# A decoder layer on one core: first three products side by side, squares summed on VectorE alone, first norm's chain with high priority

## The chip, the cores and the metric

The kernel runs on 1 core of a Trainium2 chip. The metric is device time in microseconds (us) of one execution. The engines are TensorE (PE; PEld is its weight load), VectorE (DVE), ScalarE (ACT), GpSimd (POOL) and SyncE (SP), whose queue issues the DMAs.

## The reference

One decoder layer, batch 1, 512 tokens, width 1024, all in float32:

```python
h = rms_norm(x, norm1_g[i])
proj = h @ w_in[i]
u_s5 = proj[..., :IN_S5_END]
q = proj[..., IN_S5_END:IN_Q_END]
...
z_rw = proj[..., IN_V_END:IN_RW_END]
gate_logits = proj[..., IN_RW_END:]
y_a = s5_mixer(u_s5, ...)
y_b = diff_attention(q, k, v, ...)
y_c, v_first = rwkv7_mixer(z_rw, ...)
...
merged = jnp.sum(gates * branch_out, axis=2)
x = x + (merged @ w_out[i]).astype(x.dtype)
h2 = rms_norm(x, norm2_g[i])
gu = h2 @ w_ffn_in[i]
x = x + ((jax.nn.silu(gu[..., :D_FF]) * gu[..., D_FF:]) @ w_ffn_out[i]).astype(x.dtype)
```

with `rms_norm(x, g) = x * rsqrt(mean(x*x) + eps) * g`, the mean taken over the 1024 channels of a token.

## The kernel before

Activations lie transposed, channels on the 128 partitions and the 512 tokens along the row, so x is eight tiles of 128x512. Each float32 operand is split into a high part of type float32r and the rest: `act_hi`, `act_lo` for the activations, `wh`, `wl` for a weight block of 128x512 (four k tiles of a product with 128 output columns). A product over eight k tiles is then 24 matmuls of 128x512 into one PSUM bank: hi by `wh`, lo by `wh`, hi by `wl` (lines 1296 to 1298).

The norm's scale per token isn't in `act_hi`: only the gain is multiplied in (line 252). The products start on the unscaled x, and whoever takes a product from its bank multiplies it by `R1`, the reciprocal root spread over 128 partitions: lines 330 (RWKV inputs) and 1592 (a gate). The products of the low-rank inputs, "b" and "a", are copied out of their banks first (line 329, ACT), so that their banks come free without `R1`. The two dense banks are `bank_83` and `bank_84`, so a third product waits until one of the first two has been taken.

`R1` comes from this chain: eight squares of x on ACT (line 1506); their sum in two halves, three additions on POOL and three on DVE (line 1511), and one that joins them (line 1520); eight small matmuls with a column of ones (line 1524); the reciprocal root in small DVE steps (lines 231 to 242); a copy that spreads it (line 1526); four transposes on PE (line 1529); a copy out of PSUM on ACT (line 1572).

A weight block is loaded into one of three raw tiles `wr` (SP queue, line 1224), rounded to `wh` by ACT (line 1225), and subtracted to `wl` by DVE (line 1226); only then may its raw tile be loaded again. `load4` (lines 1242 to 1254) does so for the narrow "a" weights, whose 32 columns stand four times, the third copy being the rest; that product is `narrow`, 16 matmuls on lines 1262 and 1263.

The order of the program's steps is the text `ORDER`: L is the two low-rank products, R00 the first RWKV input (the k input of pair 0), G1 a gate, R01 and R02 the next RWKV inputs, P and T an RWKV pair's preparation and its 64x64 blocks, S, H and U the S5 mixer's steps. The code issues instructions in that order, and a scheduler then orders each engine's queue once, at build time, by its own estimate of when operands are ready; on the chip every engine runs its queue in that fixed order. The tiles `x`, the squares, and S5's working tiles all come from one list of slots (`ar_6`, `ar_12` to `ar_14` among them).

Of the kernel before, what the change touches and what calls it, by code (L numbers as in the profile page):

```python
# [23 lines left out]
P = 128  # L24
T = 512
DM = 1024
DFF = 2816
KD = DM // P
# [6 lines left out]
NSPLIT = (6, 3, 2, 3)  # L35
ORDER = ("L R00 G1 R01 R02 P0 T0 I0 R10 R12 S R11 U0 P1 R20 R22 R21 T1 H0 G1 J0 U1 I1 J1 C0 P2 T2 F0 U3 U2 Q0 C1 G3 Q1 G2 H1 I2 Q2 R31 "
         "F1 R32 R30 P3 T3 J2 G1 I3 J3 C3 G1 Q3 X0 K0 A0 G2 Y0 C2 Y1 Y2 Y3 F3 X1 K1 G1 A1 F2 X2 K2 O0 O2 O3 G2 A2 X3 K3 G3 O1 A3")
# [647 lines left out]
class S5:  # L685
# [6 lines left out]
    NJ, NK, L = 16, 64, 8  # L692
# [509 lines left out]
KB = 4  # L1202


class Dense:
# [49 lines left out]

    def narrow(self, wx, nk, hi, lo, take):

        E, nc = self.E, self.E.nc
        bank = E.dense_bank()
        for k in range(nk):  # L1260
            w = wx[k // KB][:, k % KB].rearrange("p g n -> p (g n)")
            nc.tensor.matmul(bank, w, hi(k), start=k == 0, stop=False)
            nc.tensor.matmul(bank, w, lo(k), start=False, stop=k == nk - 1)
        take(bank)
        E.free(bank)

# [268 lines left out]
def trunk_kernel(ctx: ExitStack, tc: tile.TileContext, A, outT):  # L1535
# [13 lines left out]
    nc.scalar.copy(E.small("warm", [P, 1], bufs=1), E.ones)  # L1549
    norm = Rms(E, (nc.gpsimd, nc.vector))  # L1550
    with E.scope("s"):
        xs, wb = [], dense.blocks(A["w_b"], KD, P)
        for k in range(KD):
            x = E.slot("x")
            nc.sync.dma_start(x, xT[k * P:(k + 1) * P])
            E.split(x, h_hi(k), h_lo(k), E.pc("n1", k))
            xs.append(x)
            if k in (0, 2):
                dense.ahead(A["w_b"], KD, P, k // 2)
        w_a = dense.load4(A["w_a"], KD)  # L1560
        for i in range(2):
            dense.ahead(A["w_in"][4], KD, P, i)
        for k in range(KD):
            norm.add(xs[k])
# [4 lines left out]
    with E.scope("s"):  # L1569
        E.r1 = E.mpool.tile([P, 4], F32, name="r1")  # L1570
        E.R1 = E.mpool.tile([P, T], F32, name="R1")
        nc.scalar.copy(E.R1, norm(E.r1))
        E.r1sq = E.mpool.tile([P, 4], F32, name="r1sq")
        nc.vector.tensor_tensor(E.r1sq, E.r1, E.r1, ALU.mult)
# [52 lines left out]
    def lora():  # L1627
        proj(A["w_b"], lambda ps: rw.take(ps, "b"))
        dense.narrow(w_a, KD, h_hi, h_lo, lambda ps: rw.take(ps, "a"))

# [192 lines left out]
```

## Time and profile before

| what | value |
|---|---|
| median of 3 runs | 1011.51 us (1007.04 to 1014.56) |
| the profiled execution's own time | 1011.71 us |
| its span in the trace | 1009.9 us |
| PE busy | 968.3 us, 96% of the span |
| DVE busy | 753.6 us, 75% |
| ACT busy | 473.2 us, 47% |
| POOL busy | 143.8 us, 14% |

The span runs from the program's first instruction on the core to its last. PE's share is made up of matmuls that follow each other and whose ends are modelled, so 96% says that PE was seldom without work, not that it ran at its peak. A matmul's cost is best read as the distance from its start to the next one's start.

### The profile page before, as it was taken

To read this page: it belongs to the slowest core of one execution; us is meant where nothing else is said; L and a number is where in the kernel's file an instruction comes from. 1 tells how busy PE (TensorE), PEld (TensorE's weight loads), DVE (VectorE), ACT (ScalarE), POOL (GpSimd) and SP (SyncE) were. 2 spreads that over 40 slices of the span, in tenths; PEclk is the share of its full clock that TensorE was granted. 3 is DMA by queue.
4 is the path that set the end of the run, shared out by engine and by line. 5 is a ranking of instruction groups with operands and counts; after the bars stand their busy time and mean duration, and the time that the engine had idled before them with its cause. 6 is when DMAs were issued, how large, how long until landed. Compare 5 with 4: busy or idle time off the path is not lost. (4 is left out here: it accounts for less than half of the span.)

```text
span 1009.9 us, 17897 instructions
## 1 busy us (share of the span) xinstructions
PE 968.3 (96%) x6416; PEld 825.5 (82%) x6416; DVE 753.6 (75%) x1941; ACT 473.2 (47%) x978; POOL 143.8 (14%) x176
## 2 busy tenths in 40 slices
PE   6989999989999999999999899989999999999998
PEld 5767777767779787878886788889999999988886
DVE  7999666889996789977866555779989998843232
ACT  6634324424333566545455224556666666632220
POOL 3022020531420010000000332012211211000000
PEclk9999799999999999999999999989999999999999
DMA  7324252221333234252458864466667676344441
GB/s 242 116 75 112 66 121 75 74 55 53 101 106 75 79 95 126 84 157 74 152 166 282 241 206 151 143 153 159 152 160 183 143 153 169 73 149 122 136 131 37
DMA packets 105593, 129.95 MB, mean 129 GB/s; under 512 B 45376, under 2 KB 47296, under 8 KB 105504
## 3 DMA queue, kind: packets, MB, share of 16 engines
q1 hardware_dynamic: 99168, 117.28, 38.6%
q0 software_dynamic: 6336, 11.54, 7.4%
q8 instruction: 50, 0.82, 0.3%
q14 instruction: 39, 0.32, 0.1%
HBM read 109.90 MB, written 18.88 MB: 128 GB/s over the span
## 5 line engine op out<-in xcount | busy, mean ns | idle before, releaser
L1225 ACT CAST wh<-wr 128x512 fp32r<-128x512 f32 x198 | 120.3, 611 | 210.6 <-PE bank L1297 169.1
L1226 DVE TENSOR_TENSOR wl<-wr,wh 128x512 fp32r<-128x512 f32 x198 | 135.9, 689 | 81.1 <-ACT wh L1225 80.4
L1296 PE MATMUL bank<-act_hi,wh 128*128 128x512 f32 x360 | 149.3, 415 | 8.0 <-ACT wh L1225 5.9
L1297 PE MATMUL bank<-act_lo,wh 128*128 128x512 f32 x360 | 148.4, 412 | 2.0 <-DVE act_lo L253 2.0
L1298 PE MATMUL bank<-act_hi,wl 128*128 128x512 f32 x360 | 148.8, 413 | 0.0
L1385 PE MATMUL bank<-act_hi,wh 128*128 128x256 f32 x352 | 99.7, 283 | 3.4 <-ACT wh L249 3.4
L1385 PE MATMUL bank<-act_hi,wl 128*128 128x256 f32 x352 | 99.4, 283 | 0.2
L1385 PE MATMUL bank<-act_lo,wh 128*128 128x256 f32 x352 | 99.0, 282 | 0.0
L1385 PE MATMUL bank<-sp_t,wh 128*128 128x256 f32 x528 | 96.5, 283 | 0.0
L1296 PEld LDWEIGHTS bank<-act_hi,wh 128*128 128x128 f32 x360 | 69.6, 193 | 22.1 <-ACT wh L1225 5.9
L1297 PEld LDWEIGHTS bank<-act_lo,wh 128*128 128x128 f32 x360 | 69.4, 193 | 16.4 <-DVE act_lo L253 3.4
L1385 PEld LDWEIGHTS bank<-sp_t,wh 128*128 128x128 f32 x528 | 82.1, 191 | 0.0
L1298 PEld LDWEIGHTS bank<-act_hi,wl 128*128 128x128 f32 x360 | 69.4, 193 | 14.2 <-issue 0.6
L1385 PE MATMUL bank<-sp_t,wl 128*128 128x256 f32 x264 | 74.7, 283 | 0.0
L1385 PEld LDWEIGHTS bank<-act_hi,wh 128*128 128x128 f32 x352 | 67.7, 192 | 3.9 <-ACT wh L249 3.8
L1296 PE MATMUL bank<-act,wh 128*128 128x512 f32 x176 | 68.5, 389 | 0.0
L1297 PE MATMUL bank<-act,wh 128*128 128x512 f32 x176 | 68.5, 389 | 0.0
L1298 PE MATMUL bank<-act,wl 128*128 128x512 f32 x176 | 68.5, 389 | 0.0
L1385 PEld LDWEIGHTS bank<-act_hi,wl 128*128 128x128 f32 x352 | 67.4, 192 | 0.8 <-DVE wl L250 0.8
L1385 PEld LDWEIGHTS bank<-act_lo,wh 128*128 128x128 f32 x352 | 67.4, 192 | 0.0
L249 ACT CAST wh<-ar 128x512 fp32r<-128x512 f32 x79 | 48.2, 622 | 27.6 <-DMA ar<-in_w_ffn_in 13.3
L250 DVE TENSOR_TENSOR wl<-ar,wh 128x512 fp32r<-128x512 f32 x79 | 53.5, 687 | 9.1 <-ACT wh L249 7.0
(492 smaller groups left out, 2218.0 us busy)
## 6 DMA issues: line engine op xcount, KB each, us to landing
wr<-in_w_in SPq DMA_DIRECT2D x88, 256.0 KB, 3.0
ar<-in_w_ffn_in SPq DMA_DIRECT2D x46, 256.0 KB, 3.2
wr<-in_w_ffn_out SPq DMA_DIRECT2D x40, 256.0 KB, 2.7
gate<-ar SPq DMA_DIRECT2D x24, 256.0 KB, 2.5
wr<-in_w_branch SPq DMA_DIRECT2D x24, 256.0 KB, 3.3
ar<-gate SPq DMA_DIRECT2D x24, 256.0 KB, 3.4
ar<-in_w_ffn_in POOLq DMA_DIRECT2D x22, 256.0 KB, 3.9
sp_raw<-in_w_ffn_in SPq DMA_DIRECT2D x21, 256.0 KB, 3.2
```

Source lines behind the costliest of these rows:

```text
L249: nc.scalar.copy(hi, src)
L250: nc.vector.tensor_tensor(lo, src, hi.bitcast(F32), ALU.subtract)
L1225: nc.scalar.copy(wh, raw)
L1226: nc.vector.tensor_tensor(wl, raw, wh.bitcast(F32), ALU.subtract)
L1296: nc.tensor.matmul(ps, wh[:, j], hi(k), start=k == 0, stop=False)
L1297: nc.tensor.matmul(ps, wh[:, j], lo(k), start=False, stop=False)
L1298: nc.tensor.matmul(ps, wl[:, j], hi(k), start=False, stop=k == nk - 1)
L1385: nc.tensor.matmul(ps, w[x][:, c], b(y, j), start=first and j == js[0] and n == 0, stop=last and j == js[-1] and n == 2, skip_group_check= ...
```

## The change

Five edits:

- The three products of L and R00 (b, a and the k input of pair 0) run side by side in three banks: for each k tile of x there are eight matmuls, three for b, two for a, three for k. The a product takes a bank of another list, `bank_90`. Of `ORDER` only the start changes, from `L R00 G1 ...` to `L G1 ...`.
- The weights come in another order: behind the first x tile both the first b block, the a weights and the first k block; behind the fourth x tile the second b and k blocks.
- All squares are added by DVE; POOL adds none.
- The norm's chain after the sum, up to `R1`, is issued with the scheduler's highest priority.
- `narrow` goes, and `first` takes its place.

```diff
-ORDER = ("L R00 G1 R01 R02 P0 T0 I0 R10 R12 S R11 U0 P1 ...
+ORDER = ("L G1 R01 R02 P0 T0 I0 R10 R12 S R11 U0 P1 ...
...
+    def first(self, ws, wx, nk, hi, lo, takes):
+
+        nc, E = self.E.nc, self.E
+        a, b = (self.loaded.pop(repr(w)) for w in ws)
+        banks = [E.dense_bank(), E._take("ps", (P, T), True), E.dense_bank()]
         for k in range(nk):
+            q, j = k // KB, k % KB
+            first, last = k == 0, k == nk - 1
+            for bank, w in ((banks[0], a[q]), (banks[1], None), (banks[2], b[q])):
+                if w is None:
+                    x = wx[q][:, j].rearrange("p g n -> p (g n)")
+                    nc.tensor.matmul(bank, x, hi(k), start=first, stop=False)
+                    nc.tensor.matmul(bank, x, lo(k), start=False, stop=last)
+                else:
+                    nc.tensor.matmul(bank, w[0][:, j], hi(k), start=first, stop=False)
+                    nc.tensor.matmul(bank, w[0][:, j], lo(k), start=False, stop=False)
+                    nc.tensor.matmul(bank, w[1][:, j], hi(k), start=False, stop=last)
+        for bank, take in zip(banks, takes):
+            take(bank)
+            E.free(bank)
...
-    norm = Rms(E, (nc.gpsimd, nc.vector))
+    norm = Rms(E, (nc.vector,))
...
-            if k in (0, 2):
+            if k in (0, 3):
                 dense.ahead(A["w_b"], KD, P, k // 2)
-        w_a = dense.load4(A["w_a"], KD)
-        for i in range(2):
-            dense.ahead(A["w_in"][4], KD, P, i)
+                if k == 0:
+                    w_a = dense.load4(A["w_a"], KD)
+                dense.ahead(A["w_in"][4], KD, P, k // 2)
...
-        nc.scalar.copy(E.R1, norm(E.r1))
+        with tc.high_priority():
+            nc.scalar.copy(E.R1, norm(E.r1))
...
     def lora():
-        proj(A["w_b"], lambda ps: rw.take(ps, "b"))
-        dense.narrow(w_a, KD, h_hi, h_lo, lambda ps: rw.take(ps, "a"))
+
+        dense.first((A["w_b"], A["w_in"][4]), w_a, KD, h_hi, h_lo,
+                    [lambda ps: rw.take(ps, "b"), lambda ps: rw.take(ps, "a"), lambda ps: rw.take(ps, "k", 0)])
```

**PE at the start.** Before, the b product is run through and then the a product; here its end, with `wh_115` and `wl_116` the second b block and `wh_137` the first half of the a weights:

```order
L1298 MATMUL bank_83<-act_hi,wl_116 128x512
L1296 MATMUL bank_83<-act_hi,wh_115 128x512
L1297 MATMUL bank_83<-act_lo,wh_115 128x512
L1298 MATMUL bank_83<-act_hi,wl_116 128x512
L1262 MATMUL bank_84<-act_hi,wh_137 128x512
L1263 MATMUL bank_84<-act_lo,wh_137 128x512
```

Now the first rows of PE, with `wh_103` of b, `wh_110` of a and `wh_117` of k (line numbers of the changed kernel, ten or eleven higher behind `first`):

```order
L1270 MATMUL bank_83<-act_hi,wh_103 128x512
L1271 MATMUL bank_83<-act_lo,wh_103 128x512
L1272 MATMUL bank_83<-act_hi,wl_104 128x512
L1267 MATMUL bank_90<-act_hi,wh_110 128x512
L1268 MATMUL bank_90<-act_lo,wh_110 128x512
L1270 MATMUL bank_84<-act_hi,wh_117 128x512
L1271 MATMUL bank_84<-act_lo,wh_117 128x512
L1272 MATMUL bank_84<-act_hi,wl_118 128x512
```

Eight matmuls now stand on each x tile where three stood. The SP queue of the start before, where an `x8` at a row's end would be eight in a row:

```order
L1555 DMA ar_6_74<-in_xT 128x512
L1224 DMA wr_102<-in_w_b 128x512
L1555 DMA ar_6_74<-in_xT 128x512
L1555 DMA ar_12_80<-in_xT 128x512
L1224 DMA wr_114<-in_w_b 128x512
L1555 DMA ar_12_80<-in_xT 128x512 x3
L1555 DMA ar_13_81<-in_xT 128x512 x2
L1246 DMA wr_135<-in_w_a 128x256
```

The SP queue of the start now:

```order
L1565 DMA ar_6_74<-in_xT 128x512
L1224 DMA wr_102<-in_w_b 128x512
L1246 DMA wr_108<-in_w_a 128x256
L1224 DMA wr_116<-in_w_in 128x512
L1565 DMA ar_6_74<-in_xT 128x512
L1565 DMA ar_12_80<-in_xT 128x512 x2
L1224 DMA wr_102<-in_w_b 128x512
L1224 DMA wr_108<-in_w_in 128x512
L1565 DMA ar_12_80<-in_xT 128x512 x2
L1565 DMA ar_13_81<-in_xT 128x512 x2
```

The last four x tiles now stand behind two loads that use a raw tile (`wr_102`, `wr_108`) for the second time.

**DVE and ACT in the norm's chain.** DVE before, from the join of the two sums (line 1520) to the first step of the root (line 231); line 281 prepares the low-rank weights, the rest is S5's parameters:

```order
L1520 TENSOR_TENSOR ar_13_81<-ar_13_81,ar_14_82 128x512
L721 SCALAR_TENSOR_TENSOR s_r_690<-s_n_689,s_r_690 128x16
L726 TENSOR_SCALAR s_n_86_704<-s_n_689 128x16
L811 RECIPROCAL s_den_824<-s_den_824 128x16
L722 SCALAR_TENSOR_TENSOR s_r_690<-s_n_689,s_r_690 128x16
L727 TENSOR_SCALAR s_n_86_704<-s_n_86_704 128x16
L231 TENSOR_SCALAR rqx_s_178<-bank_88 128x4
L281 TENSOR_TENSOR rw_wl<-ar_1_69,rw_wl 32x1024
L233 TENSOR_SCALAR rqi_s_180<-rqx_s_178 128x4
L281 TENSOR_TENSOR rw_wl<-ar_1_69,rw_wl 32x512
```

DVE now, from the last addition (line 1521):

```order
L1521 TENSOR_TENSOR ar_13_81<-ar_13_81,ar_14_82 128x512
L281 TENSOR_TENSOR rw_wl<-ar_1_69,rw_wl 32x1024
L231 TENSOR_SCALAR rqx_s_178<-bank_88 128x4
L281 TENSOR_TENSOR rw_wl<-ar_1_69,rw_wl 32x512
L233 TENSOR_SCALAR rqi_s_180<-rqx_s_178 128x4
L1060 TENSOR_TENSOR da_pr<-da_lv 128x128
```

The long half of line 281 now stands ahead of the root's first step instead of behind it. On ACT, the rows before the copy of `R1` (line 1572) were:

```order
L1225 CAST wh_137<-wr_114 128x512
L1063 ACTIVATE da_sm<-da_sm 128x2
L1225 CAST wh_143<-wr_135 128x512
L1225 CAST wh_148<-wr_102 128x512
L1572 COPY R_172<-bank_89 128x512
```

and ahead of the same copy (line 1583) they are now:

```order
L1063 ACTIVATE da_sm<-da_sm 128x2
L329 COPY ar_7_75<-bank_90 128x512
L1225 CAST wh_117<-wr_108 128x512
L1225 CAST wh_131<-wr_116 128x512
L1225 CAST wh_136<-wr_102 128x512
L1583 COPY R_173<-bank_89 128x512
```

The copy still stands behind two weight casts whose loads are issued late, and a third cast moved behind the copy out of the a product's bank.

**PE in the second RWKV pair.** Here lines 552 and 559 are 64x64 blocks of RWKV, lines 915, 931 and 952 S5's transposes and small products. PE before:

```order
L1298 MATMUL bank_83<-act_hi,wl_140 128x512
L552 MATMUL bank_86<-ar_4_72,ar_6_74 64x64 x8
L552 MATMUL bank_86<-ar_4_72,ar_1_69 64x64 x8
L915 MATMUL bank_88<-ident,ar_14_82 128x128 x4
L931 MATMUL bank_89<-ar_14_82,s5cb_s_1788 32x128
L559 MATMUL bank_87<-ar_7_75,ar_8_76 64x32
L931 MATMUL bank_89<-ar_14_82,s5cb_s_1788 32x128 x3
L1296 MATMUL bank_84<-act_hi,wh_143 128x512
```

PE now:

```order
L1308 MATMUL bank_84<-act_hi,wl_118 128x512
L915 MATMUL bank_88<-ident,ar_13_81 128x128 x4
L915 MATMUL bank_89<-ident,ar_14_82 128x128 x4
L931 MATMUL bank_90<-ar_13_81,s5cb_s_1788 32x128 x4
L931 MATMUL bank_90<-ar_14_82,s5cb_s_1788 32x128 x4
L1306 MATMUL bank_83<-act_hi,wh_131 128x512
L1307 MATMUL bank_83<-act_lo,wh_131 128x512
L552 MATMUL bank_86<-ar_4_72,ar_6_74 64x64 x8
L552 MATMUL bank_86<-ar_4_72,ar_1_69 64x64 x8
L952 MATMUL bank_88<-ident,s_jt_874 128x128 x4
L952 MATMUL bank_89<-ident,s_jt_874 128x128 x2
```

The first of two S5 groups of lines 915 and 931, which stood far ahead of this place, has joined the second here.

## Rows read from the trace of the kernel before

**Rows 1.** The page's busy time, share of the span and instructions of each engine.

```profile
PE 968.3 (96%) x6416; PEld 825.5 (82%) x6416; DVE 753.6 (75%) x1941; ACT 473.2 (47%) x978; POOL 143.8 (14%) x176
```

**Rows 2.** Windows of 5 us: busy PE, PEld, DVE, ACT, POOL; granted clock; DMA share; GB/s.

```profile
5.00:10.00 5.00, 4.05 (x10) 2.69 (x10) 4.34 (x5) 5.00 (x10) 2.48 (x2) 1.00 1.02 355
...
40.00:45.00 5.00, 5.00 (x23) 3.99 (x22) 5.00 (x31) 1.85 (x3) 0.00 (x0) 1.00 0.22 65
```

**Rows 3.** PE in order of time: start, us, instruction, idle time before it.

```profile
5.95 0.80 PE L1296 MATMUL bank<-act_hi,wh 128*128 128x512 f32 x1 [5.95 <-ACT wh L1225]
...
9.48 0.40 PE L1298 MATMUL bank<-act_hi,wl 128*128 128x512 f32 x1
9.71 0.40 PE L1296 MATMUL bank<-act_hi,wh 128*128 128x512 f32 x1
11.40 0.50 PE L1297 MATMUL bank<-act_lo,wh 128*128 128x512 f32 x1 [1.29 <-DVE act_lo L253]
...
13.10 0.50 PE L1297 MATMUL bank<-act_lo,wh 128*128 128x512 f32 x1 [0.74 <-DVE act_lo L253]
...
20.90 0.95 PE L1524 MATMUL bank<-ones,ar 128*128 128x1 f32 x8
21.71 0.48 PE L1296 MATMUL bank<-act_hi,wh 128*128 128x512 f32 x1
...
25.99 0.40 PE L1296 MATMUL bank<-act_hi,wh 128*128 128x512 f32 x1
...
34.44 0.47 PE L1296 MATMUL bank<-act_hi,wh 128*128 128x512 f32 x1 [2.05 <-ACT ar L337]
```

**Rows 4.** ACT in order of time.

```profile
4.15 0.72 ACT L252 ACTIVATE act_hi<-ar,pcol 128x512 fp32r<-128x512 f32 x1 [1.92 <-DMA ar<-in_xT]
4.78 0.61 ACT L1506 ACTIVATE ar<-ar 128x512 f32<-128x512 f32 x1
5.29 0.60 ACT L1225 CAST wh<-wr 128x512 fp32r<-128x512 f32 x1
...
29.88 0.62 ACT L1225 CAST wh<-wr 128x512 fp32r<-128x512 f32 x1 [1.36 <-DMA wr<-in_w_in]
30.40 0.58 ACT L1572 COPY R<-bank 128x512 f32<-128x512 f32 x1
```

**Rows 5.** DVE in order of time.

```profile
8.91 1.77 DVE L1226 TENSOR_TENSOR wl<-wr,wh 128x512 fp32r<-128x512 f32 x1
...
18.94 0.69 DVE L1520 TENSOR_TENSOR ar<-ar,ar 128x512 f32<-128x512 f32 x1
...
21.88 0.16 DVE L231 TENSOR_SCALAR rqx_s<-bank 128x4 f32<-128x4 f32 x1 [1.82 <-PE bank L1524]
22.08 1.22 DVE L281 TENSOR_TENSOR rw_wl<-ar,rw_wl 32x1024 fp32r<-32x1024 f32 x1
...
27.98 0.42 DVE L1526 COPY ar<-r 128x512 f32<-128x512 f32 x1
...
33.61 0.68 DVE L1592 TENSOR_TENSOR ar<-bank,R 128x512 f32<-128x512 f32 x1
```

**Rows 6.** POOL in order of time: the second of its three additions of squares.

```profile
8.84 1.30 POOL L1511 TENSOR_TENSOR ar<-ar,ar 128x512 f32<-128x512 f32 x1 [0.40 <-ACT ar L1506]
```

**Rows 7.** Line 253 on DVE: ns min/median/max, first and last start, form.

```profile
L253 DVE SCALAR_TENSOR_TENSOR act_lo<-ar,pcol,act_hi x8: 739/744/1774, 4.9 to 14.3; 128x512 fp32r<-128x512 f32 x8
```

**Rows 8.** The eight x loads, from issue to landing.

```profile
DMA to landing us min/median/max: 2.9/4.7/5.5
```

**Rows 9.** Windows of 4 us in the second RWKV pair, columns as in rows 2.

```profile
112.00:116.00 4.00, 4.00 (x21) 2.94 (x20) 2.29 (x4) 0.58 (x1) 0.00 (x0) 0.50 0.80 194
116.00:120.00 4.00, 4.00 (x17) 3.30 (x16) 0.00 (x0) 0.66 (x2) 0.00 (x0) 0.50 0.00 0
120.00:124.00 4.00, 4.00 (x19) 2.88 (x20) 0.76 (x2) 0.83 (x2) 0.00 (x0) 0.76 0.36 81
144.00:148.00 4.00, 4.00 (x46) 3.12 (x45) 3.30 (x5) 1.18 (x2) 1.13 (x2) 1.00 0.94 185
```

More of the change, by code (lines that the diff above doesn't have):

```diff
@@ L35 @@
 NSPLIT = (6, 3, 2, 3)
-ORDER = ("L R00 G1 R01 R02 P0 T0 I0 R10 R12 S R11 U0 P1 R20 R22 R21 T1 H0 G1 J0 U1 I1 J1 C0 P2 T2 F0 U3 U2 Q0 C1 G3 Q1 G2 H1 I2 Q2 R31 "
+ORDER = ("L G1 R01 R02 P0 T0 I0 R10 R12 S R11 U0 P1 R20 R22 R21 T1 H0 G1 J0 U1 I1 J1 C0 P2 T2 F0 U3 U2 Q0 C1 G3 Q1 G2 H1 I2 Q2 R31 "
          "F1 R32 R30 P3 T3 J2 G1 I3 J3 C3 G1 Q3 X0 K0 A0 G2 Y0 C2 Y1 Y2 Y3 F3 X1 K1 G1 A1 F2 X2 K2 O0 O2 O3 G2 A2 X3 K3 G3 O1 A3")
@@ L1254, in load4 @@
         return wx
-    def narrow(self, wx, nk, hi, lo, take):
-        E, nc = self.E, self.E.nc
-        bank = E.dense_bank()
+    def first(self, ws, wx, nk, hi, lo, takes):
+        nc, E = self.E.nc, self.E
+        a, b = (self.loaded.pop(repr(w)) for w in ws)
+        banks = [E.dense_bank(), E._take("ps", (P, T), True), E.dense_bank()]
         for k in range(nk):
[L1261 to L1265, printed above, removed]
+            q, j = k // KB, k % KB
[12 more added lines that the diff above has]
+            E.free(bank)
     def tokens(self, w, nk, hi, lo, take):
@@ L1549, in trunk_kernel @@
     nc.scalar.copy(E.small("warm", [P, 1], bufs=1), E.ones)
-    norm = Rms(E, (nc.gpsimd, nc.vector))
+    norm = Rms(E, (nc.vector,))
     with E.scope("s"):
-        xs, wb = [], dense.blocks(A["w_b"], KD, P)
+        xs = []
         for k in range(KD):
```

## The prediction

> **What bounds the kernel now.** I read the page first: PE is busy for 96% of the span [rows 1], so a change can win only where PE waits or runs slowly. The change touches the first 35 us, so I went on to PE in order of time there [rows 3]. The reader is to see four losses. PE starts at 5.95 us, waiting for the first rounded weight block. From there to 9.48 us eight distances take 3.53 us, 0.44 each, where from 9.48 to 9.71 one takes 0.23: 512 columns in 0.43 us are the lower of the clock's two levels, 1.2 GHz, in 0.23 the upper, 2.4 GHz, although the granted clock of that window stands at 1.00 [rows 2]. Then come two waits for `act_lo`, 1.29 and 0.74 us. Last, at 34.44, comes a wait of 2.05 us; the trace puts it down to ACT, but PE restarts as the gate's product has been taken out of its bank, at 33.61 + 0.68 = 34.29 [rows 5]. That take needs `R1`, ready at 30.40 + 0.58 = 30.98 [rows 4], and there are 3.31 us between the two. So two things set the end of this stage: how early PE gets through b, a and k, and how early `R1` is there. Behind it VectorE is nearly full (5.00 of 5 us in a typical window, rows 2), so only a gain that both PE and VectorE get passes on.
>
> **The first products side by side.** The number of large matmuls is the same, 24 + 16 + 24 = 64. What changes is how many are ready for each x tile: eight, which take 8 x 0.233 = 1.87 us at the upper clock, where three took 0.70. ACT makes an x tile and its square in 0.63 + 0.51 = 1.14 us (the distances in rows 4), so before PE overtook it and now it can't. I rebuild the stage from these distances.
>
> ACT: the square of x0 (4.78 to 5.29) now stands behind the weight casts, so the first cast moves from 5.29 to 4.78 if its block has landed by then; PE starts between 5.95 - 0.51 = 5.44 and 5.95. I take 5.44, since the cast at 5.29 did not wait. Then three more casts and the square, 5 x 0.51 from 4.78 = 7.33, x1 at 7.96. Up to x7 there are in all 8 scalings and 10 casts and squares from 4.15: 4.15 + 8 x 0.63 + 10 x 0.51 = 14.3. `act_lo` of x7 follows 0.7 later, at 15.0.
>
> PE: 8 matmuls at the lower clock, 5.44 + 8 x 0.43 = 8.9, as x1's `act_lo` comes (7.96 + 0.7). Then 56 x 0.233 = 13.1 and the column sums of line 1524, 21.71 - 20.90 = 0.81: all three products are issued by 22.8, where this point was 25.99 before. That is 3.2 us, of which 0.5 is the earlier start and the rest the two waits, with the restart behind each. PE wants x7 only after 5.44 + 3.4 + 48 x 0.233 + 0.8 = 20.9, 5.9 us after it is ready.
>
> **The loads.** The last four x tiles are now issued behind two loads that reuse raw tiles, so SP waits until VectorE has done with the a weights, by the distances above about 6.6 us. x4 is then issued near 7.1 instead of near 4, and lands after 2.9 to 5.5 us [rows 8], at 10.0 to 12.6. ACT wants it at 4.15 + 4 x 0.63 + 9 x 0.51 = 11.3. So it costs ACT 0 to 1.3 us. PE reaches x4 at 8.9 + 3 x 1.87 = 14.5, and x4 is there at 11.3 + 0.63 + 0.7 = 12.6, so this is hidden. If that cover were gone, PE would lose what the load is late, at most 1.3.
>
> **The squares on VectorE alone.** VectorE gets three more additions of about 0.6 us and keeps four, one of which was the join: + 1.8 us. But POOL's additions weren't free. While POOL adds from 8.84 to 10.14 [rows 6], a subtraction of VectorE takes 1.77, where an addition of the same size takes 0.69 [rows 5], and one of line 253 takes 1.774 where the median is 0.744 [rows 7]: two of the three additions cost VectorE about 2.1 us, the third between 0 and 1. So the edit gives VectorE 0.3 to 1.3 us, and the two PE waits above were on that engine. The Trainium skill (Perfetto Trace Analysis, section Optimizing Scalar/DVE Operations) says that where VectorE is saturated, work may be moved to Scalar or even GPSIMD, though it doubts it between these two, which share a port; by its first half alone the edit would lose 1.8 us. The rows bear out the doubt, so I leave that loss out. Nothing else stands in POOL's queue there.
>
> The sum is complete when seven additions and VectorE's other work are done: `act_lo` of x7 at 15.0, then five additions with S5 steps between, to 18.5, against 18.94 + 0.69 = 19.63. PE reaches line 1524 after its first 51 matmuls, at 5.44 + 3.4 + 43 x 0.233 = 18.9. So VectorE is just in time; if it is late, PE's whole queue waits, and I allow 0.7.
>
> **The norm's chain.** The root's first step moves from 21.88 to 18.9 + 0.8 + 0.2 = 19.9. Behind it VectorE had 28.40 - 21.88 = 6.5 us of work up to the end of the copy of line 1526, most of it not the chain's. The long half of line 281 (1.22 us) now stands in front, in the idle time of 1.82 us. Three weight subtractions stay in the chain's way in spite of the priority, since the order was fixed before the chip's times were known. So 5.3 us, and 0.5 to 1 for a cast that now waits behind the a product's copy: 25.9. PE has its transposes behind 15 matmuls of the gate, at 22.8 + 15 x 0.233 = 26.3, done by 26.9. On ACT the copy of `R1` still stands behind two late weight casts, one of which waited 1.36 us for its load [rows 4]; its raw tile comes free near 22.7, the load takes about 3, so this cast is done at 26.3. `R1` is there at about 27.5, 3.4 us earlier. With no wait on the tile it would be 4.5 earlier, with a load that takes 4.7 [rows 8] 2.4. What is late next is the same as before: the gate's take 3.3 us behind `R1`, at 30.9. PE has issued the gate at 22.8 + 24 x 0.233 + 0.4 = 28.8 and waits about 2 us again. That wait doesn't go; it moves forward.
>
> So at the point that was 34.44 PE and VectorE are both about 3.4 us ahead (2.4 to 4.5), with the same work before them. **The sum:** 1011.71 - 3.4 = 1008.3 for the profiled execution; the median stands 0.2 below that, so 1008.1. A measurement of this kernel tells about 1% from no change, 10 us, and this is a third of it.
>
> **Rivals.**
> - *The gain is given back.* VectorE is full for the next 25 us, PE waits for RWKV's and S5's small steps, and the reordered queues cost what the start won. For it: the slots of S5's working tiles and the order of hundreds of rows changed. Against it: VectorE itself is ahead. Time: 1011.5.
> - *The reordering helps.* From 112 to 120 us the granted clock is at 0.50, and its mean of 0.76 up to 124 is another 1.9 us at that level [rows 9]. In 9.9 us PE does 5.0 us of work there. In the new order one S5 group has left the stretch ahead of that place. If the fall doesn't come, 5.0 us are won on top: 1003.1. Against it: the RWKV rows themselves stand as they did.
> - *The clock falls in a new place: slower.* In the second pair, where the window from 144 us stands at 1.00 [rows 9], two S5 groups and RWKV's blocks now stand together with two large matmuls between them, where before it was one group. A fall as long as the one at 112 us costs 5.0 - 3.4 = 1.6 more than before: 1013.1. It decides from 6.8 us at the lower clock. The Trainium skill (TensorE: Matmul & The Clock Gate, section on the HAM clock gate) says that the throttled clock is the default and that activity releases it, which speaks for this fall wherever PE's work thins out. The stretch at 112 us agrees; the same kinds of rows at 144 us ran at the upper clock, which is why its chance is small.
> - *The change doesn't do what it says:* VectorE or a load is late, PE stands at line 1524 or at x4, and the worst of the terms (0.5 start, 1.3 load, 0.7 sum) eat 2.5 of the 3.4: 1010.8. I count it with the first rival.
>
> **How the numbers follow.** Forecast (2 to 6 us faster) 0.55, gain given back or not made (within 2 us) 0.20, help from the reordering (6 us or more) 0.13, slower 0.12. The likeliest gives 1008.2, between the two sums. The range runs to both outer cases, 1002.0 to 1013.0. Faster by over 1% needs both the start's gain and more than the lost clock: 0.07. Slower by over 1% needs 13 us of new waits: 0.03. The rest is 0.90.
>
> **What would show it.** In the trace after: PE starts near 5.4 us and shows no wait for `act_lo`; VectorE's operations before 15 us take 0.7 throughout; line 1534's sums run near 19 us and `R1` is copied near 27 us; PE restarts on the third product behind the gate near 31 us, with a wait of about 2 us before. Right in the mechanism but without gain would be a start 3 us earlier and PE's work at 300 us as late as before. A start of PE later than 6 us, a wait of more than 1 us at line 1534, or a stretch of low clock that isn't in rows 9 would make the prediction wrong.

## The result and the profile after

The changed kernel takes 1019.15 us (median of 22 executions, 1011.22 to 1022.64), the kernel before 1011.44 (22 executions, 1005.59 to 1019.71). The ratio is 1.0069, 95% interval 1.0048 to 1.0091: some 7 us slower, outside the predicted range of 1002.0 to 1013.0. The profiled execution took 1020.72 us, with a span of 1018.9.

The page's busy time of the changed kernel, against [rows 1]: PE has 4.9 us more busy time for the same 6416 matmuls, in a span that is 9.0 us longer.

```profile
PE 973.2 (96%) x6416; PEld 828.6 (81%) x6416; DVE 755.3 (74%) x1944; ACT 473.1 (46%) x978; POOL 137.0 (13%) x173
```

PE in order of time at the start (columns as in [rows 3]; lines up to ten or eleven higher):

```profile
5.36 0.80 PE L1270 MATMUL bank<-act_hi,wh 128*128 128x512 f32 x1 [5.36 <-ACT wh L1225]
...
11.04 0.63 PE L1268 MATMUL bank<-act_lo,wh 128*128 128x512 f32 x1
11.46 0.44 PE L1270 MATMUL bank<-act_hi,wh 128*128 128x512 f32 x1
11.74 0.39 PE L1271 MATMUL bank<-act_lo,wh 128*128 128x512 f32 x1
...
21.12 1.02 PE L1534 MATMUL bank<-ones,ar 128*128 128x1 f32 x8 [0.58 <-DVE ar L1521]
...
25.12 0.39 PE L1306 MATMUL bank<-act_hi,wh 128*128 128x512 f32 x1
...
35.08 0.47 PE L1306 MATMUL bank<-act_hi,wh 128*128 128x512 f32 x1 [3.75 <-ACT ar L337]
```

The start is 0.59 us earlier and both waits for `act_lo` are gone, as forecast. But the spacing of 0.43 us, the lower level of the clock, holds up to 11.46, over 13 matmuls, where it ended at 9.48 before, after 8. This length isn't a mark of the kernel. In a second profile of the changed kernel (`after_again`) it ended at 10.28, after 11 matmuls, and in a kernel whose rows here are those of the kernel before (`e8_slots_only`) at 16.34, after 17:

```profile
10.28 0.40 PE L1267 MATMUL bank<-act_hi,wh 128*128 128x512 f32 x1
```

```profile
16.34 0.44 PE L1298 MATMUL bank<-act_hi,wl 128*128 128x512 f32 x1
```

In the changed kernel the gate's product begins at 25.12 and not at 22.8, and the wait behind it is 3.75 us, not 2. ACT and DVE of the changed kernel in the norm's chain, against [rows 4, 5]:

```profile
5.93 0.62 ACT L1251 CAST wh<-wr 128x512 fp32r<-128x512 f32 x1 [0.62 <-DMA wr<-in_w_a]
...
13.20 2.07 ACT L252 ACTIVATE act_hi<-ar,pcol 128x512 fp32r<-128x512 f32 x3 [0.90 <-DMA ar<-in_xT]
...
27.05 0.62 ACT L1225 CAST wh<-wr 128x512 fp32r<-128x512 f32 x1 [1.21 <-DMA wr<-in_w_in]
30.52 0.62 ACT L1225 CAST wh<-wr 128x512 fp32r<-128x512 f32 x1 [2.85 <-DMA wr<-in_w_in]
31.04 0.58 ACT L1583 COPY R<-bank 128x512 f32<-128x512 f32 x1
```

```profile
16.44 0.75 DVE L253 SCALAR_TENSOR_TENSOR act_lo<-ar,pcol,act_hi 128x512 fp32r<-128x512 f32 x1 [0.37 <-ACT act_hi L252]
...
20.29 0.69 DVE L1521 TENSOR_TENSOR ar<-ar,ar 128x512 f32<-128x512 f32 x1
21.01 1.22 DVE L281 TENSOR_TENSOR rw_wl<-ar,rw_wl 32x1024 fp32r<-32x1024 f32 x1
22.26 0.16 DVE L231 TENSOR_SCALAR rqx_s<-bank 128x4 f32<-128x4 f32 x1
...
24.96 0.69 DVE L1226 TENSOR_TENSOR wl<-wr,wh 128x512 fp32r<-128x512 f32 x1
...
27.98 0.36 DVE L1536 COPY ar<-r 128x512 f32<-128x512 f32 x1
...
34.25 0.69 DVE L1603 TENSOR_TENSOR ar<-bank,R 128x512 f32<-128x512 f32 x1
```

`R1` is there at 31.62, later than before (30.98) and not at 27.5. The sum is complete at 20.98, the root's first step comes at 22.26, and the spreading copy runs at 27.98, to the hundredth where it ran before. Then the copy out of PSUM stands on ACT behind a cast whose block landed near 30.5; its raw tile came free at 24.96 + 0.69 = 25.65, and the load issued behind that took 4.7 us. The windows of 4 us show what follows, there and at three later places (columns as in [rows 2]; the granted clock is the third number from the right):

```profile
32.00:36.00 4.00, 0.92 (x3) 0.82 (x4) 3.85 (x7) 2.96 (x6) 0.00 (x0) 0.93 0.44 131
36.00:40.00 4.00, 4.00 (x13) 3.10 (x13) 3.89 (x8) 3.78 (x7) 0.00 (x0) 0.64 0.29 98
276.00:280.00 4.00, 3.17 (x14) 2.71 (x15) 4.00 (x11) 1.52 (x3) 0.84 (x2) 0.73 0.44 117
392.00:396.00 4.00, 2.79 (x9) 2.29 (x10) 3.58 (x14) 2.44 (x9) 0.00 (x0) 0.73 0.13 46
```

None of these falls is in the profile of the kernel before, whose falls were at 112 to 122, 183, 228, 549 and 665 to 675 us; the changed kernel's other falls came at 128, 588 and 674 us. I followed the lag: how much later than before PE is when it has done the same work (each matmul counted at its line's usual distance, which makes this an estimate). At 20 us the changed kernel is 1.2 us ahead, at 45 us 2.3 behind, at 145 level (the fall of [rows 9] is in the reference), at 265 still level, at 400 8.0 behind, at 520 7.3, at the end 10.2. The spans differ by 9.0 there, so the count is good to about 1 us. So there are two large losses in this profile: some 3.5 us around the first gate, and 7 to 8 us between 265 and 400. A second profile of it on another chip had + 1.5 at 45 us, - 2.8 at 265, + 5.1 at 400, + 5.5 at the end.

### The profile page after: what moved, and what is told of

Read it like the earlier page. It is cut to its first block, busy times and chain, and to the rows that moved or that the text cites. A ratio compares the mean times of both kernels' runs of the same rounds, so it can differ in the third digit from the quotient of the medians.

```text
span 1018.9 us, 17899 instructions
## 1 busy us (share of the span) xinstructions
PE 973.2 (96%) x6416; PEld 828.6 (81%) x6416; DVE 755.3 (74%) x1944; ACT 473.1 (46%) x978; POOL 137.0 (13%) x173
## 5 line engine op out<-in xcount | busy, mean ns | idle before, releaser
L1306 PE MATMUL bank<-act_hi,wh 128*128 128x512 f32 x344 | 142.5, 414 | 6.6 <-ACT ar L337 3.8
L1307 PE MATMUL bank<-act_lo,wh 128*128 128x512 f32 x344 | 142.9, 415 | 0.0
L1308 PE MATMUL bank<-act_hi,wl 128*128 128x512 f32 x344 | 141.9, 413 | 0.0
L1306 PEld LDWEIGHTS bank<-act_hi,wh 128*128 128x128 f32 x344 | 66.5, 193 | 20.6 <-ACT ar L337 4.2
L1308 PEld LDWEIGHTS bank<-act_hi,wl 128*128 128x128 f32 x344 | 66.4, 193 | 13.4 <-issue 0.4
L1307 PEld LDWEIGHTS bank<-act_lo,wh 128*128 128x128 f32 x344 | 66.4, 193 | 12.9 <-issue 0.4
L1395 PEld LDWEIGHTS bank<-act_hi,wh 128*128 128x128 f32 x352 | 67.7, 192 | 3.2 <-ACT wh L249 3.1
L1395 PEld LDWEIGHTS bank<-act_hi,wl 128*128 128x128 f32 x352 | 67.2, 191 | 1.1 <-DVE wl L250 0.8
L1395 PEld LDWEIGHTS bank<-act_lo,wh 128*128 128x128 f32 x352 | 67.2, 191 | 0.0
```

The costliest lines, as they stand in the source:

```text
L1306: nc.tensor.matmul(ps, wh[:, j], hi(k), start=k == 0, stop=False)
L1307: nc.tensor.matmul(ps, wh[:, j], lo(k), start=False, stop=False)
L1308: nc.tensor.matmul(ps, wl[:, j], hi(k), start=False, stop=k == nk - 1)
L1395: nc.tensor.matmul(ps, w[x][:, c], b(y, j), start=first and j == js[0] and n == 0, stop=last and j == js[-1] and n == 2, skip_group_check= ...
```

## Experiments

Each run's ratio is to the kernel before on the same chip, with its 95% interval. In the order that is built, the priority moves no row of PE, DVE, ACT or SP, so two edits remain, and every kernel falls into one of three orders behind PE's row 400 (about 135 us). I call them the **old** order (that of before), the **new** one (that of the changed kernel, 706 of some 4450 PE rows elsewhere) and a **third** (407 rows from the old, 364 from the new), which the squares edit alone gives; a kernel is put with the order from which it differs by none or by up to 48 rows.

### The two halves, and one slot

Theory A: the free list of slots, which the squares edit reorders, makes the later order a slower one. Rivals B (the start carries all) and C (the additions do).

`e1_squares`, the kernel before with

```diff
-    norm = Rms(E, (nc.gpsimd, nc.vector))
+    norm = Rms(E, (nc.vector,))
```

> The kernel before with one edit alone: the three partial sums of squares that GpSimd added go to VectorE; products, loads and the start of TensorE's queue stay as they were. With this the free list of buffers after the norm comes out in another order, and with it every queue from the first mixer work on. Theory A (two pieces: about 2 us lost at the start of the changed kernel and about 5 us by the other buffers and queues later): 1.004 to 1.006 of the time before, about +5 us. Rival B (all 7 us come from the start: the first norm's factor behind a late weight block on ScalarE, the longer wait at the first gate and the low clock that follows): 0.998 to 1.001, since that start isn't made here. Rival C (the additions themselves are what costs, on a VectorE that is too late with the sum): 1.005 to 1.008, and the sum of squares is later than 18.5 us with the wait at the first gate above 3 us.

`e3_side`, the changed kernel without the priority, and with

```diff
-    norm = Rms(E, (nc.vector,))
+    norm = Rms(E, (nc.gpsimd, nc.vector))
```

> The other half alone: first three products side by side with the loads in the new order, squares still shared by GpSimd and VectorE; buffers and queues after the norm as in the kernel before. Theory A: 1.001 to 1.003, about +2 us, with a wait of more than 3 us and a low clock at the first gate, and no new loss later. Rival B: 1.005 to 1.008. Rival C: 0.997 to 1.000.

`e7_slots`, the changed kernel with two lines behind the norm, and `e8_slots_only`, the kernel before with the reverse:

```diff
+    slots = E.pools["s"].free
+    slots.insert(12, slots.pop(1))
```

> The changed kernel whole, with one buffer of the free list put back right after the norm to the place that it had in the kernel before; queues are those of the changed kernel up to the first mixer work at TensorE's row 479 of 4854, and differ behind it in some 50 rows. Theory A: 1.001 to 1.003 of the kernel before, so some 5 us faster than the changed kernel. Rival B and rival C: 1.005 to 1.008, as the changed kernel.

> The kernel before with nothing but that one buffer of the free list moved, as the squares edit moves it: the same queues up to TensorE's row 479, nothing of the change at the start. Theory A: 1.004 to 1.006, about +5 us. Rival B and rival C: 0.999 to 1.001.

Measured: `e1_squares` 0.9987 [0.9966, 1.0008], `e3_side` 0.9988 [0.9966, 1.0011], `e7_slots` 1.0059 [1.0035, 1.0083], `e8_slots_only` 0.9995 [0.9972, 1.0017]. Neither half costs anything; both together do. That refutes C, and A as far as the slot goes: moving it makes and removes nothing. It doesn't settle B, since `e3_side` has the same products side by side but not the same start: its wait at the first gate is short, and the clock holds (PE, then windows of 4 us):

```profile
34.14 0.48 PE L1306 MATMUL bank<-act_hi,wh 128*128 128x512 f32 x1 [1.81 <-ACT ar L337]
```

```profile
32.00:36.00 4.00, 2.19 (x10) 1.58 (x9) 3.81 (x8) 3.40 (x6) 0.00 (x0) 1.00 0.58 165
36.00:40.00 4.00, 4.00 (x19) 3.23 (x18) 3.89 (x12) 3.72 (x6) 0.00 (x0) 1.00 0.30 110
```

What the two have in common is that neither has the new order: `e3_side` has the old, `e1_squares` the third. A2 replaced A: the start costs some 2 us, the new order some 5, whatever brings it about.

### Start and order exchanged

`e9_r1sq_pool`: the changed kernel, the factor's square on another engine. `e5_r1_dve`: the changed kernel, `R1` copied by DVE. `e10_squares_r1_dve`: the kernel before with the squares edit and the second of these lines. `after_again`: the changed kernel once more.

```diff
-        nc.vector.tensor_tensor(E.r1sq, E.r1, E.r1, ALU.mult)
+        nc.gpsimd.tensor_tensor(E.r1sq, E.r1, E.r1, ALU.mult)
...
-        nc.scalar.copy(E.R1, norm(E.r1))
+        nc.vector.tensor_copy(E.R1, norm(E.r1))
```

> The changed kernel with one small operation on another engine: the square of the norm's factor (128x4) is made by GpSimd and not by VectorE. The start is that of the changed kernel (2 of TensorE's first 400 rows stand elsewhere); from row 400 on TensorE has row for row the order of the kernel that only has the squares edit, which ran in 0.9987 of the time before. Theory A2 (the changed kernel's order of the mixers' work behind row 400 is a slower one, +5 us, and the start costs about +2 us): 1.001 to 1.003. Rival B (the start, with the first norm's factor late on ScalarE, a wait of 3 to 4 us at the first gate and a low clock behind it, carries all): 1.005 to 1.008.

> The kernel before with the squares on VectorE and the factor R copied out of its bank by VectorE, too: the start of the kernel before (products one after the other), 8 of TensorE's first 400 rows elsewhere than in the kernel with the squares edit alone; from row 400 on TensorE has row for row the order of the changed kernel. Theory A2: 1.004 to 1.006, since the slow order comes without the changed start. Rival B: 0.997 to 1.000, since the start isn't that of the change. Rival D (the slow order costs only behind the late start): as B, with the run before this at 1.003 or less.

> The changed kernel with R copied out of its bank by VectorE and not by ScalarE, where it stands behind the cast of a weight block that lands late; from TensorE's row 400 on the order is that of the kernel with the squares edit alone. All theories: R about 1.5 to 2 us earlier than at 31.6 us, the wait at the first gate under 2.5 us, no low clock at 32 to 40 us, and 0.996 to 0.999 of the time before. A time above 1.003 would speak against A2 and B, and for the products side by side or the squares themselves.

> The changed kernel once more, for a second profile of it on the chip of these runs: 1.005 to 1.009 of the time before. Theory A2: the lag on the kernel before grows again by some 5 us between 270 and 400 us. Rival B: its lag is all there by 45 us.

Measured: `e9_r1sq_pool` 1.0040 [1.0017, 1.0064], `e10_squares_r1_dve` 1.0020 [0.9990, 1.0050], `e5_r1_dve` 1.0046 [1.0015, 1.0077], `after_again` 1.0055 [1.0027, 1.0082]. None of the first three lies in a range that was expected. The late start before the third order is slower than `e1_squares`, the new order behind the old start is not clear of no change, and `e5_r1_dve` missed: its chain ended later (the spreading copy at 28.82), so `R1` was no earlier, 31.56, the wait 2.61 us, and the granted clock 0.87 and 0.70 from 32 to 40 us. The early `R1` that it was to test didn't come about, so its 1.0046 speaks for no theory.

### R late, R early

`e11_r1_late` is the kernel before with the copy of `R1` three times; `e12_lora_pool` the changed kernel with line 281 on GpSimd; `e13_r1_early` this and `R1` copied by DVE; `e14_squares_lora` the kernel before with the squares edit and line 281 on GpSimd.

```diff
-        nc.scalar.copy(E.R1, norm(E.r1))
+        pb = norm(E.r1)
+        nc.scalar.copy(E.R1, pb)
+        nc.scalar.copy(E.R1, pb)
+        nc.scalar.copy(E.R1, pb)
...
-            nc.vector.tensor_tensor(self.wl[R, i], raw[R, i], ...
+            nc.gpsimd.tensor_tensor(self.wl[R, i], raw[R, i], ...
```

> The kernel before with nothing but a later factor R: ScalarE copies it out of its bank three times in place of once, each copy 0.58 us with other work between; the start's products, the squares and the order behind TensorE's row 400 (4 rows elsewhere) are those of the kernel before. Theory A2 (the start's part is the wait at the first gate and the low clock that follows once the wait passes some 2.5 us): R 1.2 us or more later than 30.98 us, the wait there 3.2 us or more against 2.05, a granted clock under 0.95 in 32 to 40 us, and 1.002 to 1.004 of the time before. Rival E (the changed start costs by something else, the loads or the products side by side): the wait grows, the clock may fall, but the time stays at 0.999 to 1.001.

> The changed kernel with the two subtractions of line 281 (1.22 and 0.68 us on VectorE, in among the first norm's chain) on GpSimd: the chain should end about 1.5 to 2 us earlier; R is still copied by ScalarE, behind the cast of a weight block that lands when it did. The order behind row 400 is that of the kernel before but for 29 rows. Theory A2: the slow later order is gone, and if R comes before 30.5 us with a wait under 2.5 us, the start's cost too: 0.998 to 1.001; if R still waits for the cast, a low clock at 32 to 40 us and 1.002 to 1.004. Rival E: 1.003 to 1.005 either way.

> As the run before, and R copied by VectorE, so that it waits neither for line 281 nor for a weight block's cast on ScalarE; the order behind row 400 is that of the kernel with the squares edit alone. Theory A2: R by 28 to 29 us, a wait at the first gate under 1.5 us, no low clock at 32 to 40 us, TensorE 1.5 to 2.5 us ahead of the kernel before at 40 us, and 0.996 to 0.999 of its time; this is what the change was after. Rival E: 1.001 to 1.005, though R is early.

> The squares edit alone with line 281 on GpSimd: the start of the kernel before with an earlier R, and behind row 400 the order of the changed kernel but for 48 rows. Theory A2: no low clock at 32 to 40 us, yet a lag that grows by some 5 us between 160 and 400 us as in each run with that order: 1.001 to 1.004. Rival B (the later order costs nothing): 0.996 to 0.999.

Measured: `e11_r1_late` 0.9988 [0.9963, 1.0013], `e12_lora_pool` 0.9977 [0.9955, 0.9999], `e13_r1_early` 1.0036 [1.0006, 1.0065], `e14_squares_lora` 1.0035 [1.0012, 1.0058]. Three of the four went otherwise than I had expected. In `e11_r1_late` ACT, DVE and PE in order of time show `R1` complete at 31.99, 1.0 us later than before, and PE restarting earlier than before:

```profile
31.40 0.59 ACT L1575 COPY R<-bank 128x512 f32<-128x512 f32 x1
...
33.35 0.68 DVE L1595 TENSOR_TENSOR ar<-bank,R 128x512 f32<-128x512 f32 x1
...
34.18 0.47 PE L1296 MATMUL bank<-act_hi,wh 128*128 128x512 f32 x1 [1.74 <-DVE ar L1595]
```

The gate's take follows 1.36 us behind `R1`, not the 2.63 of the kernel before (33.61 - 30.98): it has moved past line 321 and a weight subtraction in DVE's queue. So `R1` doesn't set the restart by itself. In `e12_lora_pool` the chain didn't end earlier but 3.4 us later, mostly because the last addition of squares ran beside GpSimd (DVE, then POOL; the root's first step came at 25.04 and not at 22.26):

```profile
19.39 0.69 DVE L1521 TENSOR_TENSOR ar<-ar 128x512 f32<-128x512 f32 x1
20.19 2.83 DVE L1521 TENSOR_TENSOR ar<-ar,ar 128x512 f32<-128x512 f32 x1
```

```profile
20.14 4.00 POOL L281 TENSOR_TENSOR rw_wl<-ar,rw_wl 32x1024 fp32r<-32x1024 f32 x2 [17.52 <-ACT rw_wl L279]
```

PE waited 2.90 us at line 1534, the granted clock fell to 0.50 there, and at 45 us this kernel is 3.0 us behind. Yet it has the old order, and its time is 0.9977, with an interval that ends just below 1. `e13_r1_early` is the mirror image: `R1` at 29.92 + 0.68 = 30.60, a wait of 1.61, the clock at 1.00 from 32 to 40 us, level with before at 45 us; with the third order, it is slower. `e14_squares_lora`, new order and the old products, is slower too, without a fall at the start, though PE waited there 2.63 us for the spreading copy:

```profile
28.04 0.66 PE L1529 MATMUL bank<-ident,ar 128*128 128x128 f32 x4 [2.63 <-DVE ar L1526]
```

So rival B is out: the changed start isn't needed for a loss, and a lag as large as its own isn't enough for one (`e12_lora_pool`).

### A turned bank, and the old order

`e1_again`, `e9_again` and `e10_again` repeat three runs on one chip. `e15_bank` is the changed kernel with one line behind the norm, which turns a list of three PSUM banks; `e16_bank_slot` has the slot of `e7_slots` put back as well, and `e15_again` repeats `e15_bank` beside it. Theory F: only the later order decides.

```diff
+    q_ = E.pools["ps"].free; q_.append(q_.pop(0))
```

> The squares edit alone again, beside the next two on one chip: old start, third later order. Theory A2 and rival B: 0.997 to 1.001. If it comes out at 1.003 or more, the third order costs by itself and the earlier 0.9987 was a matter of the chip.

> The changed start before the third later order, again. Theory A2 (start and order each cost): 1.002 to 1.005, above the run before this. Theory F (only the later order decides, since a start that lagged by 4 us was given back elsewhere): as the run before this within 0.002.

> The old start before the changed kernel's later order, again. Theory A2: 1.002 to 1.004, above the first run of this call. Theory F: 1.004 to 1.007, as the changed kernel. Rival B: 0.997 to 1.001.

> The changed kernel with the three banks of one PSUM free list turned by one after the norm, nothing else: products side by side, squares on VectorE; behind row 400 the order is that of the kernel before but for 29 rows (row for row that of the run with line 281 on GpSimd). Theory A2: 1.001 to 1.003 (the start's 2 to 3 us stay). Theory F: 0.997 to 1.000. Rival B: 1.005 to 1.008.

> The changed kernel with one PSUM free list turned by a bank, again. Theory A2 as it stands now (start and later order add up; here the start is 1 us ahead of before at 45 us, the order as before): 0.994 to 0.998. If the 0.9946 was chance: 0.998 to 1.000.

> As the run before, and the one buffer of the free list put back to its place in the kernel before, too: the start the same on TensorE row for row, and behind row 400 the order of the kernel before but for 4 rows on TensorE and 8 on VectorE. Theory A2: 0.994 to 0.998, no wait above 1.3 us on TensorE between 260 and 400 us, and a lag that grows there by under 2 us.

Measured: `e1_again` 0.9991 [0.9966, 1.0016], `e9_again` 1.0015 [0.9991, 1.0040], `e10_again` 1.0009 [0.9980, 1.0039], `e15_bank` 0.9946 [0.9923, 0.9970], `e15_again` 0.9972 [0.9947, 0.9996], `e16_bank_slot` 0.9979 [0.9954, 1.0004]. Three of these went otherwise than expected. `e9_again` lies below A2's range and 0.0024 above `e1_again`, where F allowed 0.002; `e10_again` lies in the range of rival B; `e15_bank` lies below all three ranges; `e1_again` and the last two lie in theirs. Theory F, that only the order decides, fails on the two pairs with the third order: `e9_r1sq_pool` and `e9_again` have a mean of 1.0028, `e1_squares` and `e1_again` of 0.9989, 0.0039 apart with an interval of some 0.0024 (an estimate from those of the runs).

One bank in a list turns the change from 1.0069 into a gain. In `e15_bank` both parts are different, and the start isn't that of the change any more, though I had expected it to be: only b and k run side by side, 48 matmuls, then come the column sums, and the a product stands behind them, its first matmul waiting until line 231 has read the sums out of their bank. DVE, ACT and PE at its start:

```profile
26.86 0.41 DVE L1536 COPY ar<-r 128x512 f32<-128x512 f32 x1
...
28.02 0.59 ACT L1583 COPY R<-bank 128x512 f32<-128x512 f32 x1 [0.81 <-PE bank L1539]
29.19 0.63 ACT L1225 CAST wh<-wr 128x512 fp32r<-128x512 f32 x1 [0.58 <-PE bank L1307]
...
20.87 0.95 PE L1534 MATMUL bank<-ones,ar 128*128 128x1 f32 x8
22.07 0.50 PE L1267 MATMUL bank<-act_hi,wh 128*128 128x512 f32 x1 [0.25 <-DVE rqx_s L231]
...
33.16 0.47 PE L1306 MATMUL bank<-act_hi,wh 128*128 128x512 f32 x1 [0.97 <-DVE ar L1604]
```

Here the copy of `R1` stands ahead of the cast and runs as soon as PE has its transposes: `R1` is there at 28.61, PE restarts at 33.16, 1.28 us ahead of before, and the clock holds. And behind row 400 it has the old order. So these three runs don't show the change with another order: their gain belongs to a start and an order together. PE's rows with a wait above 0.9 us between 260 and 400 us, of `e15_bank`:

```profile
277.93 0.66 PE L265 MATMUL bank<-ident,ar 128*128 128x128 f32 x4 [0.92 <-DVE ar L263]
359.73 0.49 PE L619 MATMUL bank<-rw_Z,ar 128*128 128x128 f32 x2 [0.98 <-DVE rw_Z L646]
381.47 0.49 PE L619 MATMUL bank<-rw_Z,ar 128*128 128x128 f32 x2 [1.19 <-DVE rw_Z L646]
```

and the same of the changed kernel, with the matmuls behind the last wait:

```profile
276.83 1.02 PE L258 MATMUL bank<-const,ar 128*128 128x2 f32 x8 [1.80 <-DVE ar L672]
...
370.52 0.49 PE L619 MATMUL bank<-rw_Z,ar 128*128 128x128 f32 x2 [1.17 <-DVE rw_Z L646]
393.21 0.50 PE L1306 MATMUL bank<-act_hi,wh 128*128 128x512 f32 x1 [2.81 <-ACT ar L1115]
393.54 0.38 PE L619 MATMUL bank<-rw_Z,ar 128*128 128x128 f32 x2
393.68 0.63 PE L1307 MATMUL bank<-act_lo,wh 128*128 128x512 f32 x1
394.10 0.63 PE L1308 MATMUL bank<-act_hi,wl 128*128 128x512 f32 x1
```

The new order has two longer waits, 1.80 us for RWKV's last step (line 672) and 2.81 us for a bank that ACT empties (line 1115); the spacing of 0.42 us behind the second is the lower level of the clock. All six profiles with the new order have both waits, 1.79 to 1.81 and 2.80 to 2.87; in five of them the clock also fell behind one or both (in `e10_squares_r1_dve` behind neither). The six with the third order have one wait of 1.12 to 1.15 us at line 258 near 270 us, and five of them a fall there. With the old order nothing in this stretch waits longer than 1.2 us, and seven of eight profiles have no fall in it. In these profiles the falls go with the order, not simply with the length of the wait: 1.12 us was enough in the third order, 1.19 us in the old one was not.

### All runs side by side

The lag at 45 us and its growth from 145 to 520 us, both against the profile of before, one profile each. The lag at 45 us holds the draw of the first matmuls' clock, too: the + 2.1 of `e8_slots_only` comes with the 17 slow matmuls above.

| kernel | lag at 45 us | order | growth | ratio |
|---|---|---|---|---|
| `e8_slots_only` | + 2.1 | old | - 1.4 | 0.9995 |
| `e11_r1_late` | - 0.1 | old | - 0.1 | 0.9988 |
| `e3_side` | - 0.2 | old | + 4.2 | 0.9988 |
| `e12_lora_pool` | + 3.0 | old | - 0.7 | 0.9977 |
| `e15_bank`, `e15_again` | - 1.1, - 1.3 | old | + 2.0, + 1.3 | 0.9946, 0.9972 |
| `e16_bank_slot` | - 1.4 | old | + 0.9 | 0.9979 |
| `e1_squares`, `e1_again` | - 0.4, - 1.7 | third | + 3.0, + 5.7 | 0.9987, 0.9991 |
| `e13_r1_early` | + 0.3 | third | + 3.8 | 1.0036 |
| `e5_r1_dve` | + 2.0 | third | + 3.0 | 1.0046 |
| `e9_r1sq_pool`, `e9_again` | + 2.3, + 2.9 | third | + 2.6, + 5.1 | 1.0040, 1.0015 |
| `e10_squares_r1_dve`, `e10_again` | - 1.6, - 2.1 | new | + 7.5, + 11.1 | 1.0020, 1.0009 |
| `e14_squares_lora` | + 0.3 | new | + 6.2 | 1.0035 |
| `e7_slots` | + 3.2 | new | + 7.2 | 1.0059 |
| changed kernel, `after_again` | + 2.3, + 1.5 | new | + 7.6, + 7.2 | 1.0069, 1.0055 |

The mean growth is 0.9 us with the old order, 3.9 with the third and 7.8 with the new; with each matmul counted at its median distance over all the profiles, single entries move by up to 2 us and the means are 0.3, 4.1 and 7.5. The mean ratios are 0.9978, 1.0019 and 1.0041.

Four corners are the cleanest reading, two starts before two orders. With the third order they are 0.9989 (the start near that of before, lag - 1.1) and 1.0028 (the changed start, + 2.6), with the new order 1.0015 (- 1.9) and 1.0061 (mean of three, + 2.3). The start makes 0.0039 and 0.0046, the order 0.0026 and 0.0033; only the 0.0026 isn't clear of the noise. So before these two orders start and order add up, to about the 0.0069 of the change. It isn't a rule for all rows of the table: with the old order `e12_lora_pool` (+ 3.0) and `e16_bank_slot` (- 1.4) are 0.0002 apart, and `e13_r1_early` (third, + 0.3) is as slow as rows that lag by 2 us. No run has the changed start unaltered before the old order.

## Why the prediction was wrong

**What bounds the kernel now** named the right four losses. The start at 5.36, the end of the two waits for `act_lo` and the restart behind the gate's take were as described.

**The first products side by side** failed in one term above all: 8 matmuls at the lower clock, where the trace has 13. Five more at 0.43 in place of 0.233 are 1.0 us; with the wait of 0.58 at line 1534 that is 1.6 of the 25.12 - 22.8 = 2.3 us that were missing. The gain was 0.9 us, not 3.2. The number 8 came from one execution and differs from one to the next: the second profile of the changed kernel has 11 and begins the gate at 24.41, 1.6 us early. Taking it for a property of the kernel was the error, and how much it cost in each profile is a draw.

**The squares on VectorE alone** was right in its mechanism. Line 253 takes 743 to 753 ns throughout, where its slowest took 1774 [rows 7], and `e1_squares` brings the root's first step forward from 21.88 to 20.58 at no cost. Most of these 1.3 us are a matter of order, since four matmuls (0.93 us) moved behind the column sums; the sum itself is complete at 19.34, where it was at 19.63. The Trainium skill (Perfetto Trace Analysis, section Optimizing Scalar/DVE Operations) doubts that moving work between VectorE and GPSIMD helps, since they share a port; the trace agrees, in `e12_lora_pool` with 2.83 us for an addition of 0.69.

**The loads** were hidden from PE, as forecast, but not from the norm. ACT waited 0.62 us for the a weights and 0.90 for x4 (forecast 0 to 1.3), `act_lo` of x7 was done at 17.19 and not at 15.0, and the five additions behind it ended at 20.98 and not at 18.5. I had counted this delay on PE's path alone.

**The norm's chain** is the step that failed first: forecast was `R1` at 27.5, measured 31.62. Of these 4.1 us, 2.4 are the late sum (the root's first step at 22.26 and not at 19.9). On DVE the chain took 28.34 - 22.26 = 6.1, where I had 6.0 at 25.9 - 19.9. The other 1.8 are ACT's queue: PE's transposes were done at 29.23, but the copy of `R1` stood until 31.04 behind the late weight block, whose raw tile came free at 25.65 and not near 22.7 and whose load took 4.7 us and not 3; why this load was slower than the 3.0 us of its like in `e15_bank` stays open. `e15_bank`, with only two products side by side and the copy ahead of that cast, has `R1` at 28.61 and PE 1.28 us ahead of before: an earlier `R1` does bring PE forward, there by a third of the forecast.

**"That wait doesn't go; it moves forward"** failed with it. The 3.3 us from `R1` to the end of the gate's take held in the changed kernel (34.25 + 0.69 - 31.62 = 3.32). But PE came 0.9 us earlier and the take 0.64 later, so the wait grew from 2.05 to 3.75, and the clock, which I had priced only in the second pair, fell behind it, as it did in all six profiles of the four kernels with this start, with waits of 2.61 to 3.94 us. Nor is the distance fixed: it is the order of DVE's queue, from `R1` to the start of the take 2.63 us here, 1.36 in `e11_r1_late` and 3.72 in `e15_bank`. From - 3.4 the term became + 2.3 at 45 us.

**The rivals.** I had looked at the new order at one place only, the stretch from 112 us, and let it cost nothing or give 5 us. The profiles put some 7 us at places where I compared no rows, 276 and 393 us; by the times, the new order costs 0.0033, some 3 us, more than the third behind the same start. "The gain is given back" had the mechanism, with too small a price; "the clock falls in a new place" had the other half of it, at the wrong place. The two rivals on the clock, "the reordering helps" and "the clock falls in a new place", were priced on the fall of [rows 9], which belongs to that one execution: `e8_slots_only` and `e11_r1_late`, whose rows there are those of the kernel before, have none at 112 us. Neither edit costs by itself, and with all three products side by side, the squares on VectorE and the old order (`e12_lora_pool`, with line 281 on GpSimd) the time is 0.9977: so the loss isn't a fixed price of what the change does. That `e15_bank`, `e15_again` and `e16_bank_slot` come out near the 1008.2 that I forecast (0.9946, 0.9972 and 0.9979) is no proof of my sum, since they reach it by another start. The priority, which I took to move little, moves nothing.

**What stays open.** Why the scheduler builds a new order from so small a difference wasn't tried. Why the third order is 0.4% slower behind some starts and not behind that of `e1_squares` isn't fully told by a lag of 1 to 4 us, and a late start before the old order showed no cost. The stretch of 265 to 400 us is shown as the place by profiles of single executions; that the waits of 1.80 and 2.81 us are the cause, apart from everything else in that order, was not isolated.

## What to carry to other kernels

Where a scheduler orders the queues, a small edit at the start draws a new order for everything behind it, and that draw can cost as much as the edit was to win (here some 3 us between two orders behind one start, by the times, and up to 7 by the profiles, against 3.4): compare the built orders over the whole program, look for rows that have lost the work that hid them, and judge an edit on several orders before judging its idea (a turned free list gives one, but look whether it has changed the edit's own rows as well). A number that one profile shows, such as a count of slow matmuls or a fall of the clock, has to be looked for in a second profile before it becomes a term of a sum. A gain that brings one engine sooner to the same late operand only lengthens a wait, and here the clock fell behind the longer wait as well. A chain is as late as the last thing ahead of it in each queue that it passes: here a cast on ScalarE for a load issued too late.

## What the hardware showed

- The lower level of the clock at the start lasted from 5.95 to 9.48 us before (8 matmuls) and from 5.89 to 16.34 in `e8_slots_only` (17), which has the same rows there; from 5.36 to 11.46 in the changed kernel (13) and from 5.29 to 10.28 in its second profile (11). The Trainium skill (TensorE: Matmul & The Clock Gate, section on the HAM clock gate) describes such a slow start of a run of matmuls; the rows agree that there is one, and show that its length differs between executions of the same rows.
- In the set of runs of `after_again` the kernel before had a mean granted clock of 0.9905 and a mean time of 1010.6 us, the changed kernel 0.9867 and 1015.7. Between executions of one kernel the time falls by about 0.80 us for each 0.001 of that clock, so by this slope an estimated 3.8 x 0.80 = 3.0 of the 5.1 us between them go with the clock, the rest with waits.
- The length of a wait alone doesn't tell whether the clock falls: there was no fall behind 2.63 us in `e14_squares_lora` or 1.19 us in `e15_bank`, and one behind 2.61 us in `e5_r1_dve` and 1.12 us in `e13_r1_early`. Falls vary between executions of the same kernel: 340 us had one in the second profile of the changed kernel and none in the first.
- A 128x512 addition on VectorE took 2.83 us beside a GpSimd subtraction of 4.00 us for two pieces, and that subtraction took 1.22 + 0.68 on VectorE.
